# Turning softmax weights by VectorE and memory instead of by TensorE, in a two-layer decoder trunk

## The chip, the cores and the metric

The kernel runs on one NeuronCore of a Trainium2 chip. The metric is the device time of one execution in microseconds (us), the lower the better. Engines are named as in the profile: PE (TensorE, matrix products; PEld its weight loads), DVE (VectorE), ACT (ScalarE), POOL (GpSimd, which here only issues transfers), SP (which issues the transfers of the model's weights).

## The reference

Two layers over 256 tokens of width 2048, in fp32. The first layer has stick-breaking attention, the second, to which the change belongs, has dilated window attention in three groups of four heads over keys and values that are shared:

```
scores = einsum('brnqhd,brnkhd->brnhqk', qb, kb) * (dh ** -0.5)
scores = where(valid[:, None], scores, -inf)
m = max(scores, axis=-1);  e = exp(scores - m);  den = sum(e, axis=-1)
o = einsum('brnhqk,brnkhd->brnqhd', e / den, vb)
lse = m + log(den)
...
alpha = softmax(stack(lses, axis=2), axis=2)
o = stack(outs, axis=2) * alpha[..., None]
return o.reshape(b, s, B_WIDTH) @ w_o
```

So each head's output is its unscaled weights `e` times the values, times one factor per token, head and group (alpha over the denominator), and the 12 heads (1536 columns) go through `w_o`. After each attention follow a gated feed-forward block with a short convolution (5632 wide) and a gated addition of a per-layer embedding.

## The kernel before, in words

**Strips.** Every large product is made in strips of 512 output columns. `strip_v` keeps a strip in two PSUM banks, one for each half of the tokens (t = 0, 1), and for every block of 128 inputs and each half makes three products of 128x512: fp32 is rebuilt from a high and a low part of both sides (L346, L347, L348). A strip over 16 blocks is 96 such products. The model's weights come 1 MB at a time (`raw`, four buffers), and for every pair of blocks ScalarE writes the high part (`whi`, L303) and VectorE the low part (`wlo`, L304), with four buffers of each and priority over other work; a new pair can be written when TensorE is through with the pair four before.

**What sets the order.** The program is written without waits; a scheduler decides the order on each engine from the dependences, from the priorities and from `tc.issue_after`, which puts an instruction behind a given other one. Engines execute in that order.

**Turning.** A strip `u` with tokens on the partitions is turned (`turn_out`, `turn_in`) by VectorE in squares of 32x32 (L241), written to memory by POOL (`there<-y`, L244: two transfers of 256 KB) and read back with the squares rearranged (`turned<-there`, L252: four of 128 KB). The kernel does this for queries, keys and activations.

**The attention of the second layer** (`mixer_b`). Queries of groups 0 and 1, keys of groups 0 and 1, then `weights_of(0)`, queries of group 2, `weights_of(1)`, keys of group 2, values of group 0, `weights_of(2)`. `weights_of(g)` copies the turned queries into one run each on ScalarE (`in_one_run`, L487), makes the scores on TensorE into a double bank `two` (one buffer, queries of the second half) and a bank `keys` (first half), and for each head VectorE takes the maximum (L612, L613) and ScalarE the exponential (L614) into `e`, queries on the partitions, 384 columns: 256 for the second half of the queries, 128 for the first. Then a few small operations give the factors `co` (L637 to L649).

`weights_turned(g)` scales the four heads' `e` by `co` (L656), turns them on TensorE by 12 products with the identity `idf` (called through `one_run`, which is L406 in the profile), and copies the three banks out (L665, `aT`). `pv` multiplies: values are stationary, turned weights move; the result has the head's columns on the partitions, and is split into high and low parts as blocks `o` for the next product (L151, L152). This goes group by group between the strips of the values, and the strips of `wo_b` (12 blocks, 72 products each) follow in `add_strips`.

`products` makes a list of strips. With `late`, the first two strips are begun with the blocks that exist, `late()` is issued within the second of them to make the last four blocks, and then both are completed; in the kernel before, `wo_b` has no `late`.

Of the kernel before, what the change touches and what calls it, by code (L numbers as in the profile page):

```python
# [72 lines left out]
def tile_trunk(ctx, tc, head_d, xT_d, x_d, pT_d, pos_d, vec_d, cst_d, csb_d, wqkv, wo_a, wkv, wq_b, wo_b, wup, wdn, wpg, wpp, gfin_d, out_d):  # L73
# [277 lines left out]
    def products(jobs, xs, late=None, at=0, then={}):  # L351
# [6 lines left out]
        if late is not None:  # L358
            n = len(xs)

            def before(k0):
# [7 lines left out]
                strip_v(W, s, xs[:n], base, ends=False, before=(lambda k0: None, before)[i])  # L369
                for i, (W, s, base) in enumerate(jobs[:2])  # L370
# [3 lines left out]
            jobs = jobs[2:]  # L374
# [199 lines left out]
    def mixer_b(xs, late, hkv_of, rc):  # L574
# [15 lines left out]
        def weights_of(g):  # L590
            q, k = in_one_run(qs[g]), ks[g]
            gm = cbf[:, B_GM + g * S : B_GM + (g + 1) * S]
            two, one = two_banks(), bank("keys0")
            with one_run() as product:
# [10 lines left out]
                product(one.rearrange("p (h c) -> p h c", h=HG), IDB, mask, start=False, stop=True)  # L605
            for h in range(HG):
# [8 lines left out]
                es.append(e)  # L615
# [36 lines left out]
        def weights_turned(g):  # L652
            two, one = two_banks(), bank("keys1")
            for h, e in enumerate(es[g * HG : (g + 1) * HG]):
                for b, sl in ((1, slice(0, S)), (0, slice(S, S + P))):
                    nc.vector.tensor_scalar(e[:, sl], e[:, sl], co[:, b, g, h : h + 1], None, op0=OP.mult)  # L656
            with one_run() as product:
                for h in (3, 2, 1, 0):
                    e = es[g * HG + h]
                    keys0 = two[:, h // 2, (h % 2) * S : (h % 2 + 1) * S]  # L660
                    for out, c in ((keys0[:, :P], S), (keys0[:, P:], 0), (one[:, h * P : (h + 1) * P], P)):
                        product(out, e[:, c : c + P], idf, is_transpose=True, start=True, stop=True)
            ts = [rt("aT") for _ in range(3)]
            for t, d in zip(ts, (two[:, 0], two[:, 1], one)):
                nc.vector.tensor_copy(t, d)  # L665
            return [(ts[h // 2][:, (h % 2) * S : (h % 2 + 1) * S], ts[2][:, h * P : (h + 1) * P]) for h in range(HG)]

        heads = weights_turned(0)
        for g in range(NG):
            os += pv(heads, vs[g])  # L670
            if g + 1 < NG:
                heads = weights_turned(g + 1)
# [296 lines left out]
```

## Time and profile before

| | us |
|---|---|
| median of three runs | 2319.91 (2319.89 to 2320.4) |
| the profiled execution's own time | 2320.16 |
| its span, first to last instruction | 2318.4 |
| PE busy | 2303.9 |
| DVE, ACT, POOL busy | 1485.6, 1258.2, 267.6 |

Busy time counts an instruction from its start to its end; on TensorE successive products overlap, so the time that one takes from the next is read from the distance of their starts. A row of a timeline is: start, duration, engine, line, operation, output and inputs with buffer numbers left out, how many were merged, and in brackets the idle time before it and what ended it. The scores of the second layer's attention lie at 1297, 1322 and 1369 us of the span, the groups of products that the change removes at 1389, 1401 and 1414.

### The profile page before, as it was taken

Reading aid. Unit: us, or ns where it says so; the run is one execution under the profiler, and the core shown is the slowest. Engines: PE = TensorE matmul, PEld = TensorE weight load, DVE = VectorE, ACT = ScalarE, POOL = GpSimd, SP = SyncE. Lnnn points to the kernel's source line nnn. Section 1 sums busy time; section 2 is a strip of 40 time slices with the busy share of each in tenths; the row PEclk is TensorE's granted clock in tenths of the full one; section 3 lists DMA queues with packets and bytes.
Section 4 is the critical chain, followed back from the end, with each engine's and each line's share of the span. In section 5 each row is a group of like instructions: output and inputs, shape, how many; then the busy total and the mean of one; then the engine's idle time right before and its main releaser. Section 6 shows DMA issues by size and latency. Waiting matters only on the chain.

```text
span 2318.4 us, 27676 instructions
## 1 busy us (share of the span) xinstructions
PE 2303.9 (99%) x10268; PEld 1904.5 (82%) x10268; DVE 1485.6 (64%) x2110; ACT 1258.2 (54%) x1679; POOL 267.6 (12%) x466
## 2 busy tenths in 40 slices
PE   9999999999999999999999999999999999999998
PEld 7888888888888888888888888888888888888886
DVE  7555556677754767765677666667775476776565
ACT  6555545555544555545566544555553455654554
POOL 0100001111100111101011100211110011110100
PEclk9999999999999999999999999999999999999999
DMA  8656557677756777767677654867775677776763
GB/s 292 223 206 222 198 192 247 237 244 246 237 188 209 241 237 247 240 206 246 218 247 244 220 198 164 262 240 245 241 232 198 204 242 242 240 244 206 241 225 118
DMA packets 92168, 523.34 MB, mean 226 GB/s; under 512 B 14848, under 2 KB 15232, under 8 KB 40064
## 3 DMA queue, kind: packets, MB, share of 16 engines
q1 hardware_dynamic: 62352, 434.93, 53.3%
q0 software_dynamic: 27104, 80.77, 12.3%
q10 hardware_dynamic: 2576, 5.87, 0.7%
q8 instruction: 80, 1.31, 0.2%
q14 instruction: 56, 0.46, 0.1%
HBM read 479.04 MB, written 42.47 MB: 225 GB/s over the span
## 4 chain that ended last, share of the span: by engine, by line
PE 99%; DVE 0%; DMA 0%; ACT 0%; issue 0%; SPq 0%; DVEq 0%
PE accv L348 32%; PE accv L347 32%; PE accv L346 32%; PE two L406 2%; PE acc L330 1%; PE acc L333 0%; PE two L347 0%; PE two L346 0%; PE two L348 0%; DMA raw<-in_wqkv 0%; PE keys L406 0%; ACT whi L303 0%; DVE e L656 0%; DVE wlo L304 0%; ACT sq L215 0%
## 5 line engine op out<-in xcount | busy, mean ns | idle before, releaser
L304 DVE TENSOR_TENSOR wlo<-raw,whi 128x1024 fp32r<-128x1024 f32 (+1 forms) x821 | 1001.8, 1221 | 750.2 <-ACT whi L303 749.5
L303 ACT ACTIVATE whi<-raw 128x1024 fp32r<-128x1024 f32 (+1 forms) x821 | 867.4, 1058 | 908.8 <-PE accv L348 881.3
L348 PE MATMUL accv<-whi,h 128*128 128x512 f32 x2288 | 891.7, 390 | 0.0
L347 PE MATMUL accv<-wlo,h 128*128 128x512 f32 x2288 | 891.1, 389 | 0.0
L346 PE MATMUL accv<-whi,h 128*128 128x512 f32 x2288 | 890.5, 389 | 0.0
L348 PEld LDWEIGHTS accv<-whi,h 128*128 128x128 f32 x2288 | 429.5, 188 | 89.2
L347 PEld LDWEIGHTS accv<-wlo,h 128*128 128x128 f32 x2288 | 429.5, 188 | 88.9
L346 PEld LDWEIGHTS accv<-whi,h 128*128 128x128 f32 x2288 | 429.5, 188 | 88.8
L346 PE MATMUL accv<-whi,g 128*128 128x512 f32 x704 | 273.9, 389 | 0.0
L347 PE MATMUL accv<-wlo,g 128*128 128x512 f32 x704 | 273.9, 389 | 0.0
L348 PE MATMUL accv<-whi,g 128*128 128x512 f32 x704 | 273.9, 389 | 0.0
L244 POOL DMA_DIRECT2D there<-y x154 | 87.1, 566 | 1541.4 <-DVE y L241 1530.4
L252 POOL DMA_DIRECT2D turned<-there x308 | 180.3, 592 | 413.9 <-DMA there<-y 256.7
L347 PEld LDWEIGHTS accv<-wlo,g 128*128 128x128 f32 x704 | 132.1, 188 | 27.5
L346 PEld LDWEIGHTS accv<-whi,g 128*128 128x128 f32 x704 | 132.1, 188 | 27.5
L348 PEld LDWEIGHTS accv<-whi,g 128*128 128x128 f32 x704 | 132.1, 188 | 27.3
L346 PE MATMUL accv<-whi,o 128*128 128x512 f32 x224 | 87.4, 390 | 0.0
L348 PE MATMUL accv<-whi,o 128*128 128x512 f32 x224 | 87.3, 390 | 0.0
L347 PE MATMUL accv<-wlo,o 128*128 128x512 f32 x224 | 87.2, 389 | 0.0
L241 DVE STREAM_TRANSPOSE y<-u 128x512 f32<-128x512 f32 x114 | 80.3, 705 | 5.1 <-ACT u L383 2.6
L710 DVE SCALAR_TENSOR_TENSOR val<-turned,vec,val 128x248 f32<-128x248 f32 (+1 forms) x176 | 72.3, 462 | 0.0
L710 DVE SCALAR_TENSOR_TENSOR gate<-turned,vec,gate 128x240 f32<-128x240 f32 (+1 forms) x176 | 72.2, 461 | 0.0
(181 smaller groups left out, 1157.1 us busy)
## 6 DMA issues: line engine op xcount, KB each, us to landing
raw<-in_wup SPq DMA_DIRECT2D x176, 1024.0 KB, 5.2
raw<-in_wdn SPq DMA_DIRECT2D x88, 1024.0 KB, 4.9
raw<-in_wqkv SPq DMA_DIRECT2D x44, 1024.0 KB, 5.2
there<-y POOLq DMA_DIRECT2D x154, 256.0 KB, 3.9
turned<-there POOLq DMA_DIRECT2D x308, 128.0 KB, 4.9
raw<-in_wpg SPq DMA_DIRECT2D x32, 1024.0 KB, 4.9
raw<-in_wkv SPq DMA_DIRECT2D x24, 1024.0 KB, 5.1
raw<-in_wo_a SPq DMA_DIRECT2D x16, 1024.0 KB, 4.9
```

The lines of the kernel that those rows point to most:

```text
L241: last["turned"] = nc.vector.transpose(y.rearrange("p (b o r) -> p o b r", b=4, o=4), strip.rearrange("p (o b c) -> p o b c", o=4, b=4)).ins
L244: nc.gpsimd.dma_start(there[t * P : (t + 1) * P], y)
L252: nc.gpsimd.dma_start(z[32 * b : 32 * b + 32].rearrange("p a o r -> p a (o r)"), back[b])
L303: last["high"] = nc.scalar.activation(hi[:, c], r, AF.Copy).ins
L304: last["low weights"] = nc.vector.tensor_tensor(lo[:, c], r, f32(hi[:, c]), op=OP.subtract).ins
L330: nc.tensor.matmul(ps[o], hi[:, c], xs[k], start=k == 0, stop=False)
L346: nc.tensor.matmul(ps[t], xl, hi, start=k == 0 and not begun, stop=False)
L347: nc.tensor.matmul(ps[t], xh, lo, start=False, stop=False)
L348: nc.tensor.matmul(ps[t], xh, hi, start=False, stop=ends and k == n - 1)
L406: run.append(nc.tensor.matmul(*args, skip_group_check=True, **kw).ins)
L710: nc.vector.scalar_tensor_tensor(c, z[:, :, o, : 32 - d], taps(2 - d, j + o), c, op0=OP.mult, op1=OP.add)
```

## The change

The exponentials `e` are no longer scaled and no longer turned on TensorE. VectorE turns them in squares of 32x32 right after each head's exponentials (three operations a head, into three tiles `y`: the first and second half of the keys for the second half of the queries, and the keys of the first half), POOL writes each tile to memory (three transfers of 256 KB) and reads it back (twelve of 64 KB), and ScalarE copies each into one run per head (`weights_in_one_run`). For groups 0 and 1 these copies come at the head of the next `weights_of`, for group 2 behind the evacuation of the second strip of values.

In `values`, which replaces `pv`, the turned weights are stationary and the values move, 12 products of 128 columns a group, with queries on the partitions of the result. VectorE multiplies the result by `co` on its way out of PSUM, and the strip is turned through memory like the others; `split` then makes the `o` blocks from what came back. The last group's blocks are the `late` of `wo_b`, which begins three strips with the eight blocks of groups 0 and 1 before it completes them; the third lies in the double bank.

```diff
     def split(src, h):
-        nc.scalar.activation(h[:, :S], src, AF.Copy)
-        last["low"] = nc.vector.tensor_tensor(h[:, S:], src, f32(h[:, :S]), op=OP.subtract).ins
+        high, low = like(h[:, :S], src), like(h[:, S:], src)
+        nc.scalar.activation(high, src, AF.Copy)
+        last["low"] = nc.vector.tensor_tensor(low, src, f32(high), op=OP.subtract).ins
...
-    def products(jobs, xs, late=None, at=0, then={}):
+    def products(jobs, xs, late=None, at=0, then={}, side=2):
...
-                strip_v(W, s, xs[:n], base, ends=False, before=(lambda k0: None, before)[i])
-                for i, (W, s, base) in enumerate(jobs[:2])
+                strip_v(
+                    W,
+                    s,
+                    xs[:n],
+                    base,
+                    ends=False,
+                    before=before if i == side - 1 else lambda k0: None,
+                    room=two_banks() if i == 2 else None,
+                )
+                for i, (W, s, base) in enumerate(jobs[:side])
...
         def weights_of(g):
+            if g > 0:
+                weights_in_one_run(g - 1)
             q, k = in_one_run(qs[g]), ks[g]
...
+            ys = [rt("y") for _ in range(3)]
...
-                es.append(e)
+                squares = e[:, : 3 * P].rearrange("p (k b r) -> p k b r", k=3, b=4)
+                for k in range(3):
+                    y = ys[k].rearrange("p (b h r) -> p h b r", b=4, h=HG)
+                    nc.vector.transpose(y[:, h], squares[:, k])
+            zs = []
+            for y in ys:
+                there = dram.tile([P, 512], F32, tag="weights", bufs=3, name=nm("there"))
+                nc.gpsimd.dma_start(there, y)
+                zs.append((rt("turned"), there))
+            for z, there in zs:
+                back = there.rearrange("(a c) (b f) -> b c a f", c=32, b=4)
+                for b in range(4):
+                    nc.gpsimd.dma_start(z[32 * b : 32 * b + 32].rearrange("p (a f) -> p a f", a=4), back[b])
+            es.append([z for z, _ in zs])
+
+        def weights_in_one_run(g):
...
+            for z in es[g]:
+                r = rt("run")
+                with tc.issue_after(last["out"]), tc.issue_after(last["high"]):
+                    nc.scalar.activation(
+                        r.rearrange("p (h a r) -> p h a r", h=HG, r=32), z.rearrange("p (a h r) -> p h a r", h=HG, r=32), AF.Copy
+                    )
+                out.append(r)
+            es[g] = out
...
-        def weights_turned(g):
-            two, one = two_banks(), bank("keys1")
-            for h, e in enumerate(es[g * HG : (g + 1) * HG]):
-                for b, sl in ((1, slice(0, S)), (0, slice(S, S + P))):
-                    nc.vector.tensor_scalar(e[:, sl], e[:, sl], co[:, b, g, h : h + 1], None, op0=OP.mult)
...
-                    for out, c in ((keys0[:, :P], S), (keys0[:, P:], 0), (one[:, h * P : (h + 1) * P], P)):
-                        product(out, e[:, c : c + P], idf, is_transpose=True, start=True, stop=True)
...
-        heads = weights_turned(0)
-        for g in range(NG):
-            os += pv(heads, vs[g])
...
+        def values(g, v):
...
+                for t, parts in ((1, ((w[1], v[1]), (w[0], v[0]))), (0, ((w[2], v[0]),))):
+                    for i, (wt, vt) in enumerate(parts):
+                        for h in (3, 2, 1, 0):
...
+                            product(po[:, t, c], wt[:, c], vt[:, c], start=first, stop=final)
...
+                nc.vector.tensor_tensor(heads(u), heads(po[:, t]), c, op=OP.mult)
...
+            return turn_in(turn_out(us))
...
+        z = values(0, vs[0])
+        vs.append(scaled(strip_v(wkv, NG + 1, hkv), rc, lambda: rt("v")))
+        weights_in_one_run(2)
+        zs = [z, values(1, vs[1])]
+
+        def before(k0):
+            if k0 == len(hkv) - 2:
+                with tc.issue_after(last["high"]), tc.issue_after(last["low weights"]):
+                    use(zs[0])
+
+        vs.append(scaled(strip_v(wkv, NG + 2, hkv, before=before), rc, lambda: rt("v")))
+        with tc.issue_after(last["out"]), tc.issue_after(last["low weights"]):
+            use(zs[1])
+        z = values(2, vs[2])
+        return os, lambda: use(z)
...
-        h, late = add_strips(wo_a if i == 0 else wo_b, o, G_FFN + i * KB, norm)
+        h, late = add_strips(wo_a if i == 0 else wo_b, o, G_FFN + i * KB, norm, late=o_late, at=4, side=3)
```

How this moves instructions is read from the order on each engine. The first place is TensorE at group 0's weights (in these rows a name ends with its tile's number; L406 is the line of `one_run` before and L415 after, L346 to L348 become L347 to L349). Before, the end of a value strip, the turning products and, 14 products later, the value products:

```order
L348 MATMUL accv_10931<-whi_11024,h_9789 128x512
L406 MATMUL two_10841<-idf,e_10252 128x128 x2
L406 MATMUL keys_1982_10842<-idf,e_10252 128x128
L406 MATMUL two_10841<-idf,e_10245 128x128 x2
L406 MATMUL keys_1982_10842<-idf,e_10245 128x128
L406 MATMUL two_10841<-idf,e_10238 128x128 x2
L406 MATMUL keys_1982_10842<-idf,e_10238 128x128
L406 MATMUL two_10841<-idf,e_10231 128x128 x2
L406 MATMUL keys_1982_10842<-idf,e_10231 128x128
L346 MATMUL accv_10924<-whi_11040,h_9792 128x512
```

After, at the corresponding place:

```order
L347 MATMUL accv_11003<-whi_11078,h_9721 128x512
L348 MATMUL accv_11003<-wlo_11079,h_9721 128x512
L415 MATMUL two_10961<-v_10852,run_10461 128x128 x4
L415 MATMUL two_10961<-v_10850,run_10459 128x128 x4
L415 MATMUL two_10961<-v_10850,run_10463 128x128 x4
L349 MATMUL accv_11003<-whi_11078,h_9721 128x512
L347 MATMUL accv_11003<-whi_11078,h_9724 128x512
```

The turning products and their two PSUM tiles are gone, and the value products stand alone between strip products.

The second place is ScalarE ahead of the scores of group 1. Before, the strip of group 2's queries is evacuated (`u`, L383) and the queries of group 1 are copied into runs:

```order
L303 ACTIVATE whi_10508<-raw_10506 128x1024
L383 ACTIVATE u_10397<-accv_10265,rq_9478 128x512
L303 ACTIVATE whi_10524<-raw_10506 128x1024
L383 ACTIVATE u_10399<-accv_10272,rq_9478 128x512
L487 ACTIVATE run_10423<-turned_9879 128x256 x2
L487 ACTIVATE run_10426<-turned_9879 128x256 x2
L303 ACTIVATE whi_10542<-raw_10540 128x1024
```

After:

```order
L392 ACTIVATE u_10435<-accv_10308,rq_9478 128x512
L648 ACTIVATE run_10459<-turned_10276 128x512
L648 ACTIVATE run_10461<-turned_10279 128x512
L304 ACTIVATE whi_10620<-raw_10618 128x1024
L304 ACTIVATE whi_10636<-raw_10618 128x1024
L648 ACTIVATE run_10463<-turned_10282 128x512
L496 ACTIVATE run_10465<-turned_9879 128x256 x2
L496 ACTIVATE run_10468<-turned_9879 128x256 x2
L304 ACTIVATE whi_10654<-raw_10652 128x1024
```

Three copies of weights that came back from memory, and two more weight pairs, now stand ahead of the query copies (L487, now L496).

The third place is TensorE at the scores that wait for these copies. Before, they stand behind the second product of the strip's second weight pair (`whi_10490`; the strip's first is `whi_10472`):

```order
L348 MATMUL accv_10483<-whi_10472,h_9590 128x512
L346 MATMUL accv_10476<-whi_10490,h_9593 128x512
L347 MATMUL accv_10476<-wlo_10491,h_9593 128x512
L406 MATMUL two_10429<-turned_10207,run_10426 128x256
L406 MATMUL keys_1914_10430<-turned_10207,run_10426 128x128
```

After, they stand behind the first product of its fourth pair (`whi_10602`; the pairs are `whi_10550`, `whi_10568`, `whi_10586`, `whi_10602`):

```order
L349 MATMUL accv_10561<-whi_10586,h_9602 128x512
L347 MATMUL accv_10554<-whi_10602,h_9709 128x512
L415 MATMUL two_10471<-turned_10207,run_10468 128x256
L415 MATMUL keys_1926_10472<-turned_10207,run_10468 128x128
L415 MATMUL two_10471<-turned_10207,run_10468 128x256
```

A pair is 12 products, so the scores moved from behind 14 products of the strip to behind 37, 23 later. In the same way the scores of group 2 stand 11 strip products later than before. From the end of `wo_b`'s third strip on, TensorE's order is that of before.

More of the change, by code (lines that the diff above doesn't have):

```diff
@@ new lines, in use @@
+        def use(z):
+            for h in range(HG):
+                o = rt("o", dt=F32R)
+                split(z[:, :, h], o)
+                os.append(o)
+        z = values(0, vs[0])
[6 more added lines that the diff above has]
+                    use(zs[0])
```

32 lines of the change are left out of this document (16 added, 16 removed).

## The prediction

> **What bounds the kernel now.** I read the page's busy shares and its chain of work first, then TensorE's waits, then its timeline around the lines that the change touches.
>
> ```profile
> PE 2303.9 (99%) x10268; PEld 1904.5 (82%) x10268; DVE 1485.6 (64%) x2110; ACT 1258.2 (54%) x1679; POOL 267.6 (12%) x466
> ...
> PE 99%; DVE 0%; DMA 0%; ACT 0%; issue 0%; SPq 0%; DVEq 0%
> ```
>
> TensorE (PE) carries the end: the chain that ended last is TensorE for 99%. Its waits, in us in total, times, longest:
>
> ```profile
> PE acc L330 <- DVE h L146: 2.0, 3, 1.2
> PE warm L127 <- DVE zero L124: 1.2, 1, 1.2
> PE two L406 <- DVE e L656: 0.2, 1, 0.2
> ```
>
> Only the last lies in the changed part. So a microsecond is won only where TensorE gets less to do, and lost where it meets a wait it did not have; VectorE, ScalarE and GpSimd count only through such a wait. The windows say how much room they have (columns: TensorE, weight loads, VectorE, ScalarE, GpSimd, granted clock, DMA share, GB/s):
>
> ```profile
> 1310.00:1330.00 20.00, 20.00 (x95) 16.46 (x94) 12.94 (x27) 10.82 (x22) 2.46 (x5) 1.00 0.54 188
> ...
> 1390.00:1410.00 20.00, 20.00 (x106) 17.02 (x105) 15.12 (x32) 7.10 (x12) 0.00 (x0) 1.00 0.44 159
> ```
>
> **What the removed turning costs TensorE.** The timeline of TensorE (start, duration) around the three groups; durations overlap, so I use starts:
>
> ```profile
> 1388.39 0.39 PE L348 MATMUL accv<-whi,h 128*128 128x512 f32 x1
> 1388.99 0.41 PE L406 MATMUL two<-idf,e 128*128 128x128 f32 x2 [0.21 <-DVE e L656]
> ...
> 1390.56 0.39 PE L347 MATMUL accv<-wlo,h 128*128 128x512 f32 x1
> ...
> 1393.32 0.39 PE L347 MATMUL accv<-wlo,h 128*128 128x512 f32 x1
> 1393.55 2.78 PE L406 MATMUL two<-aT,v 128*128 128x128 f32 x16
> ...
> 1396.40 0.40 PE L346 MATMUL accv<-whi,h 128*128 128x512 f32 x1
> ...
> 1401.17 0.39 PE L346 MATMUL accv<-whi,h 128*128 128x512 f32 x1
> ...
> 1403.11 0.40 PE L348 MATMUL accv<-whi,h 128*128 128x512 f32 x1
> ...
> 1406.07 0.39 PE L346 MATMUL accv<-whi,h 128*128 128x512 f32 x1
> ...
> 1409.14 0.40 PE L348 MATMUL accv<-whi,h 128*128 128x512 f32 x1
> ...
> 1413.69 0.39 PE L347 MATMUL accv<-wlo,h 128*128 128x512 f32 x1
> ...
> 1415.51 0.40 PE L346 MATMUL accv<-whi,h 128*128 128x512 f32 x1
> ...
> 1424.59 0.39 PE L347 MATMUL accv<-wlo,o 128*128 128x512 f32 x1
> ...
> 1427.85 0.40 PE L346 MATMUL accv<-whi,o 128*128 128x512 f32 x1
> ```
>
> The pace of the strips comes from 1396.40 to 1401.17: 21 products, 0.227 us each. The first strip product behind an insertion starts before the pipeline has settled, so I go to the second one, two paces on. The 12 turning products of group 0 cost 1390.56 - 1388.39 - 2 x 0.227 = 1.72 us (with the 0.21 of waiting), of group 1 1403.11 - 1401.17 - 0.45 = 1.49, of group 2 1415.51 - 1413.69 - 0.45 = 1.37. All 36 go: **-4.57 us**. Their VectorE neighbours (L656, L665) go too, which frees no time of TensorE beyond that wait.
>
> The value products cost in the same way 2.63, 2.62 and 2.81 us. Before, 8 products of 128 or 256 columns, 1536 columns in all, each in two passes (the x16). After: 12 products of 128 columns, the same 1536, in 24 passes. Equal columns give +0. The turning products are passes of 128 columns too: (1390.56 - 0.23 - 1388.99)/12 = 0.112 each, and 24 of these are 2.69, 0.07 more. Could the weight loads hold short passes up? One lasts 0.188 (the last number but one in its group's row is the mean in ns):
>
> ```profile
> L348 PEld LDWEIGHTS accv<-whi,h 128*128 128x128 f32 x2288 | 429.5, 188 | 89.2
> ```
>
> Held up, the eight short passes of before would take 1.5 us, and with 0.22 for each long one the group 3.3; it took 2.62, and with 0.112 and 0.22 it is 2.69. So they don't. I take **+0.15** for three groups, between 0 and +0.21. The extra 0.19 of group 2 (its wait for values or weights) may go or stay: I let it stay.
>
> VectorE's turning against TensorE's is where a page of the Trainium skill speaks against the change: "VectorE: DVE Perf Modes", Rules for kernel authors, advises TensorE for a full 128x128 turn where PSUM will do as its goal, and The three transpose paths gives 390 ns for it there. By that price the 36 would be worth 14.0 us (an estimate), and the time 2306.9; the three stretches above contain all 36 and hold 4.57, and the measurement decides. That the other way costs more than it saves is rival C.
>
> **A new wait before the scores of group 1.** The weights of group 0 now go VectorE, memory, back, and three ScalarE copies. The new order puts these copies ahead of the copies of the queries that the scores of group 1 wait for, and these scores 23 strip products later. What stood there before, in TensorE's timeline (scores of group 0, scores of group 1, the second strip product behind them) and ScalarE's:
>
> ```profile
> 1297.43 0.64 PE L406 MATMUL two<-turned,run 128*128 128x256 f32 x2
> ...
> 1322.54 0.64 PE L406 MATMUL two<-turned,run 128*128 128x256 f32 x2
> ...
> 1326.09 0.40 PE L346 MATMUL accv<-whi,h 128*128 128x512 f32 x1
> ```
> ```profile
> 1309.03 0.19 ACT L614 ACTIVATION_READ_ACCUMULATOR e<-keys,nmx 128x1 f32 x1
> ...
> 1319.57 1.06 ACT L303 ACTIVATE whi<-raw 128x1024 fp32r<-128x1024 f32 x1 [0.67 <-PE accv L348]
> 1320.54 0.67 ACT L383 ACTIVATE u<-accv,rq 128x512 f32<-128x512 f32 x1
> 1321.10 1.33 ACT L487 ACTIVATE run<-turned 128x256 f32<-128x256 f32 x4
> 1322.33 1.05 ACT L303 ACTIVATE whi<-raw 128x1024 fp32r<-128x1024 f32 x1
> ```
>
> TensorE reaches the scores at 1322.54 + 23 x 0.227 = 1327.76. ScalarE, from 1321.10: two copies of 128x512 from SBUF (0.62 each by the row below), a weight pair that TensorE frees at 1322.33, the next one at 1322.33 + 12 x 0.227 = 1325.05, done at 1326.1, the third copy to 1326.7, and the four query copies to 1328.0; before, TensorE started 0.11 behind them (1321.10 + 1.33 to 1322.54). So 1328.1, a wait of **0.35** even if memory is never late.
>
> ```profile
> L215 ACT ACTIVATE sq<-x 128x512 f32<-128x512 f32 x48 | 29.9, 623 | 1.1 <-DVE x L821 0.4
> ```
>
> Is it late? The rows for the way through memory, before, in GpSimd's timeline, VectorE's group of such turns, and the landing of transfers into the turned tiles between 1300 and 1360:
>
> ```profile
> 1298.79 0.56 POOL L244 DMA_DIRECT2D there<-y  x1 [2.19 <-DVE y L241]
> 1303.25 2.34 POOL L252 DMA_DIRECT2D turned<-there  x4 [3.90 <-DMA there<-y]
> ...
> 1451.57 2.35 POOL L252 DMA_DIRECT2D turned<-there  x4 [5.16 <-DMA there<-y]
> ```
> ```profile
> L241 DVE STREAM_TRANSPOSE y<-u 128x512 f32<-128x512 f32 x114 | 80.3, 705 | 5.1 <-ACT u L383 2.6 <-DMA there<-y 2.2
> ```
> ```profile
> DMA to landing us min/median/max: 2.7/3.2/5.4
> ```
>
> The last exponentials ended at 1309.2. VectorE now turns three 128x128 squares for each of four heads: a quarter of the row's 0.705 is 0.18, and a fixed part makes it more; I take 0.27, so 0.8 a head and at most 3.2 in all, part of it in VectorE's idle time: ready at 1311 to 1312.4, taken 1311.6. The first copy out to the first copy back is 4.46 us (1298.79 to 1303.25), and up to 0.56 + 5.16 = 5.7 in the busier row: 1316.1. Twelve issues back at 2.34/4 = 0.585: the last begins at 1322.5 and lands 2.7 to 5.4 later (the pieces are half the bytes), 3.2 in the middle: 1325.7 against the 1326.1 at which ScalarE gets there. Hidden, then, by a margin of 0.4 only; with the long values 1316.1 + 1.3 + 6.4 + 5.4 = 1329.2, 3.1 over. The earlier two tiles, waited for too, can push the two weight pairs by up to 1 us. I take **0.7** for the whole wait, with ends 0 and 3.4. What queues behind the waiting copies on ScalarE are weight pairs; TensorE needs the next one only after the scores and 11 strip products (1326.09 - 0.23 - 1322.54 + 11 x 0.227 = 5.8 us), so they starve nothing below some 5 us.
>
> **Scores of group 2.** They stand 11 strip products later, and three copies and one weight pair go ahead of the query copies:
>
> ```profile
> 1367.98 1.32 ACT L487 ACTIVATE run<-turned 128x256 f32<-128x256 f32 x4
> ```
> ```profile
> 1369.42 0.64 PE L406 MATMUL two<-turned,run 128*128 128x256 f32 x2
> ```
>
> TensorE: 1369.42 + 11 x 0.227 = 1371.92. ScalarE: 1367.98 + 3 x 0.57 + 1.0 + 1.32 + 0.11 = 1372.1. **+0.2**, between 0 and 0.5. Memory is no part of it: from scores to return the way of group 0 takes 1325.7 - 1297.4 = 28 us, and the scores of groups 1 and 2 lie 44 apart. Those of group 2 have 175 strip products, 40 us, before their weights are used.
>
> **What I cost at nothing.** (1) The outputs' way (scaling by VectorE out of PSUM, turn, memory, splits): those of groups 0 and 1 have a whole strip of 96 products (21.8 us) and more; those of group 2 have three strips of 8 blocks, 144 products, 32.7 us, against about 1.4 + 1.4 + 4.5 + 2.3 + 5.4 + 2 = 17. Without that cover each us over is a us of TensorE. (2) The third strip takes the double bank, free once group 2's products are scaled, 16 us before. (3) Strips 0 to 2 of wo end 5.4 us apart instead of 16.3, so VectorE's additions and turns bunch; weight pairs go ahead of them in both queues, and the fourth strip (72 products, 16.3 us) takes the rest. (4) The extra traffic, 9 x 0.5 + 3 x 1 MB over 130 us, is 58 GB/s on DMA engines busy for 0.44 to 0.54.
>
> **Sum:** -4.57 + 0.15 + 0.7 + 0.2 = -3.5 us. The profiled execution took 2320.16, so 2316.6; it lies 0.25 above the median 2319.91, so a median of **2316.4**. A measurement tells about 0.2% (4.6 us) from no change: faster begins at 2315.3, slower at 2324.6.
>
> **Rivals.** *A, memory is late* (13%): the scores of group 1 wait 2 to 4 us, as with the long values above; for it speaks that twelve small pieces follow each other on one queue where the row has four; against it the median. 2317.7 to 2319.7. One sentence on its cause: "SBUF — State Buffer", SBUF: two separate sides, says that some VectorE operations lock GpSimd out from writing descriptors; GpSimd's issues above, 0.56 to 0.59 each beside a VectorE busy for 64%, show none of it. *B, nothing is late* (9%): no new wait, equal products, and group 2's 0.19 gone: -4.57 - 0.19 = -4.8, 2315.2. Against it speaks the copy chain, which is longer by more than the 23 products without memory. *C, slower* (4%): the same copies on ScalarE as in A, but the return so late that weight pairs starve behind it. Every us beyond 1326.1 costs one: the gain is eaten by a return at 1330.0 (-4.57 + 0.15 + 0.35 + 0.2 = -3.9), and a loss of over 4.6 needs 1334.6, a landing of 12 us where the longest seen took 5.4. There TensorE also runs out of weight pairs. 2324.6 and more. That the turning is still on TensorE can't be: the order of after has none of its rows.
>
> **Chances.** Forecast (2315.3 to 2317.7) 74%, A 13%, B 9%, C 4%. Range: from B's 2315.1 to A's 2318.8, leaving out the end of A and C. Faster by over 0.2%: B and the forecast's lowest end, 0.11. Slower: 0.04. Same: 0.85.
>
> **What would show it.** No products with idf on TensorE; each group of value products at 2.6 to 2.9 us; a gap of 0.3 to 1.5 us before the scores of group 1, released by a ScalarE run copy, and one under 0.5 before group 2's; none at the o blocks of wo. It is wrong if TensorE waits anywhere else, above all for weight pairs behind a late copy, or if the scores of group 1 wait over 2 us.

## The result and the profile after

| | us |
|---|---|
| before, median of 4 runs | 2320.15 (2319.89 to 2320.96) |
| after, median of 4 runs | 2334.16 (2332.43 to 2336.05) |
| after over before | 1.0061, 95% interval 1.0049 to 1.0073 |
| the profiled execution of after | 2336.05, span 2333.9 |
| predicted | 2316.4 |

The change made the kernel slower by 14 us. The busy shares and the chain of work in the page of after:

```profile
PE 2306.9 (99%) x10256; PEld 1906.7 (82%) x10256; DVE 1488.5 (64%) x2125; ACT 1262.6 (54%) x1688; POOL 302.8 (13%) x529
...
PE 96%; DMA 2%; DVE 1%; issue 0%; ACT 0%; POOL 0%; SPq 0%; DVEq 0%; ACTq 0%; POOLq 0%
```

TensorE is still the bound, but DMA now has 2% of the chain, so something in memory sets the end for a while. What TensorE waited for in after (total, times, longest, in us):

```profile
PE two L415 <- ACT run L496: 6.7, 1, 6.7
PE two L415 <- DMA turned<-there: 5.2, 1, 5.2
```

L415 is what L406 was. These two single waits stand before the scores of group 1 and of group 2. TensorE's timeline of after at both places:

```profile
1329.56 0.39 PE L347 MATMUL accv<-whi,h 128*128 128x512 f32 x1
1336.63 1.22 PE L415 MATMUL two<-turned,run 128*128 128x256 f32 x2 [6.69 <-ACT run L496]
...
1338.08 1.06 PE L415 MATMUL two<-turned,run 128*128 128x256 f32 x2
...
1343.11 0.39 PE L349 MATMUL accv<-whi,h 128*128 128x512 f32 x1
...
1383.50 0.39 PE L347 MATMUL accv<-whi,h 128*128 128x512 f32 x1
1389.10 1.19 PE L415 MATMUL two<-turned,run 128*128 128x256 f32 x2 [5.21 <-DMA turned<-there]
...
1394.94 0.39 PE L349 MATMUL accv<-whi,h 128*128 128x512 f32 x1
```

Two losses at each place. The pause: 1336.63 - 1329.56 - 0.23 = 6.8 us and 1389.10 - 1383.50 - 0.23 = 5.4. And the pace behind it: from the scores' start to the second strip product behind them 6.48 us in group 1 and 5.84 in group 2, where the kernel before needed 1326.09 - 1322.54 = 3.55; that is 2.9 and 2.3 more. The windows of after show why (columns as before):

```profile
1330.00:1336.00 6.00, 0.00 (x0) 0.00 (x0) 2.08 (x2) 3.88 (x8) 1.42 (x3) 0.69 0.44 145
1336.00:1344.00 8.00, 7.37 (x24) 5.94 (x25) 2.32 (x6) 1.89 (x4) 2.34 (x4) 0.59 0.74 197
1344.00:1354.00 10.00, 10.00 (x45) 8.26 (x44) 8.24 (x27) 6.32 (x20) 0.05 (x1) 1.00 0.28 107
...
1389.00:1395.00 6.00, 5.91 (x21) 4.96 (x22) 0.31 (x1) 0.00 (x0) 0.00 (x0) 0.60 0.25 105
```

The granted clock falls while TensorE stands still (0.69 over the first pause), averages 0.59 and 0.60 of full speed over the scores that follow, and is 1.00 again behind them. It is at half from 1332.31 to 1342.55 and from 1386.92 to 1393.75; the rows are in the last section.

The sum: 6.8 + 2.9 + 5.4 + 2.3 = 17.4 us lost at the scores. Behind the scores of group 2 the kernel is 3.8 us shorter than before: its last product comes 928.07 us after the last product of those scores, 934.39 in before, and 11 strip products (2.5 us) have moved ahead of them. The scores of group 0 begin 2.0 us later (1299.46 against 1297.43), from waits at the start of the kernel that the change doesn't touch. 17.4 - 3.8 + 2.0 = 15.6, and the profiled executions differ by 15.9.

What the first pause waited for, in ScalarE's timeline of after:

```profile
1329.56 0.63 ACT L648 ACTIVATE run<-turned 128x512 f32<-128x512 f32 x1 [6.33 <-DMA turned<-there]
1332.32 0.63 ACT L648 ACTIVATE run<-turned 128x512 f32<-128x512 f32 x1 [2.12 <-DMA turned<-there]
1332.85 1.99 ACT L304 ACTIVATE whi<-raw 128x1024 fp32r<-128x1024 f32 x2
1334.74 0.61 ACT L648 ACTIVATE run<-turned 128x512 f32<-128x512 f32 x1
1335.26 1.32 ACT L496 ACTIVATE run<-turned 128x256 f32<-128x256 f32 x4
```

ScalarE stands at the copies of group 0's weights (L648), and the query copies (L496) that the scores need stand behind them; the releaser is a transfer into `turned`. GpSimd's timeline of after shows the way through memory, and for group 1 what came behind it:

```profile
1313.61 1.65 POOL L634 DMA_DIRECT2D there<-y  x3 [6.08 <-DVE y L630]
1320.52 4.36 POOL L639 DMA_DIRECT2D turned<-there  x8 [5.26 <-PE accv L349]
1328.14 2.17 POOL L639 DMA_DIRECT2D turned<-there  x4 [3.25 <-DMA turned<-there]
...
1361.26 4.36 POOL L639 DMA_DIRECT2D turned<-there  x8 [5.64 <-DMA there<-y]
1367.82 2.17 POOL L639 DMA_DIRECT2D turned<-there  x4 [2.20 <-PE accv L349]
1369.98 1.11 POOL L245 DMA_DIRECT2D there<-y  x2
1378.33 2.34 POOL L253 DMA_DIRECT2D turned<-there  x4 [7.24 <-DMA there<-y]
```

Out to back took 6.9 us: the first transfer out landed 6.3 us after its issue, and the return was issued 0.6 later. (The return's row names TensorE, which ended a product just then; with the same three tiles in the kernel before, below, the row names the transfer.) Then eight of the twelve pieces were issued, GpSimd waited 3.3 us until an earlier one had landed, and the last four followed. The keys of group 2 (L245, L253) are issued without idle time behind the weights of group 1. They had been standing behind them, for VectorE had turned their second half by 1360.6, 9.4 us before the first of these issues:

```profile
1359.88 0.71 DVE L242 STREAM_TRANSPOSE y<-u 128x512 f32<-128x512 f32 x1
```

They were back at 1389.

### The profile page after: what moved, and what is told of

It reads as the page before. It is cut to its first block, busy times and chain, and to the rows that moved or that the text cites. A ratio compares the mean times of both kernels' runs of the same rounds, so it can differ in the third digit from the quotient of the medians.

```text
span 2333.9 us, 27792 instructions
## 1 busy us (share of the span) xinstructions
PE 2306.9 (99%) x10256; PEld 1906.7 (82%) x10256; DVE 1488.5 (64%) x2125; ACT 1262.6 (54%) x1688; POOL 302.8 (13%) x529
## 4 chain that ended last, share of the span: by engine, by line
PE 96%; DMA 2%; DVE 1%; issue 0%; ACT 0%; POOL 0%; SPq 0%; DVEq 0%; ACTq 0%; POOLq 0%
PE accv L347 30%; PE accv L348 30%; PE accv L349 30%; PE two L415 2%; DMA turned<-there 1%; DMA there<-y 1%; PE acc L331 1%; PE two L347 0%; PE two L348 0%; PE two L349 0%; PE acc L334 0%; DMA raw<-in_wqkv 0%; PE keys L415 0%; POOL turned L253 0%; ACT whi L304 0%
## 5 line engine op out<-in xcount | busy, mean ns | idle before, releaser
L348 PE MATMUL accv<-wlo,h 128*128 128x512 f32 x2288 | 891.3, 390 | 0.0
L349 PE MATMUL accv<-whi,h 128*128 128x512 f32 x2288 | 891.2, 390 | 0.0
L347 PE MATMUL accv<-whi,h 128*128 128x512 f32 x2288 | 890.5, 389 | 0.1
L347 PEld LDWEIGHTS accv<-whi,h 128*128 128x128 f32 x2288 | 429.5, 188 | 89.3 <-DVE h L146 0.5
L349 PEld LDWEIGHTS accv<-whi,h 128*128 128x128 f32 x2288 | 429.5, 188 | 89.1
L348 PEld LDWEIGHTS accv<-wlo,h 128*128 128x128 f32 x2288 | 429.4, 188 | 89.1 <-issue 0.2
L245 POOL DMA_DIRECT2D there<-y x160 | 90.6, 567 | 1430.4 <-DVE y L242 1408.4
L347 PE MATMUL accv<-whi,g 128*128 128x512 f32 x704 | 273.9, 389 | 0.0
L348 PE MATMUL accv<-wlo,g 128*128 128x512 f32 x704 | 273.9, 389 | 0.0
L349 PE MATMUL accv<-whi,g 128*128 128x512 f32 x704 | 273.9, 389 | 0.0
L253 POOL DMA_DIRECT2D turned<-there x320 | 187.6, 593 | 439.2 <-DMA there<-y 222.1
L349 PEld LDWEIGHTS accv<-whi,g 128*128 128x128 f32 x704 | 132.1, 188 | 27.6
L347 PEld LDWEIGHTS accv<-whi,g 128*128 128x128 f32 x704 | 132.1, 188 | 27.4
L348 PEld LDWEIGHTS accv<-wlo,g 128*128 128x128 f32 x704 | 132.1, 188 | 27.3
L347 PE MATMUL accv<-whi,o 128*128 128x512 f32 x200 | 78.0, 390 | 0.0
L349 PE MATMUL accv<-whi,o 128*128 128x512 f32 x200 | 77.9, 389 | 0.0
L348 PE MATMUL accv<-wlo,o 128*128 128x512 f32 x200 | 77.8, 389 | 0.0
```

Of the source, the lines that this page charges most:

```text
L245: nc.gpsimd.dma_start(there[t * P : (t + 1) * P], y)
L253: nc.gpsimd.dma_start(z[32 * b : 32 * b + 32].rearrange("p a o r -> p a (o r)"), back[b])
L347: nc.tensor.matmul(ps[t], xl, hi, start=k == 0 and not begun, stop=False)
L348: nc.tensor.matmul(ps[t], xh, lo, start=False, stop=False)
L349: nc.tensor.matmul(ps[t], xh, hi, start=False, stop=ends and k == n - 1)
```

## The experiments

Theory Q: the whole loss is two queues, ScalarE's (query copies behind copies whose weights are late) and GpSimd's (keys behind weights). Rival D: the DMA engines are full, so whatever the order, something is late. Rival S: the scores are slow of themselves. "Before" beside each is from runs on the same chip.

**The copies later, the keys first, both.**

```diff
         def weights_of(g):
-            if g > 0:
-                weights_in_one_run(g - 1)
             q, k = in_one_run(qs[g]), ks[g]
...
             es.append([z for z, _ in zs])
+            if g > 0:
+                weights_in_one_run(g - 1)
```

> One edit to the kernel after: the copies of group g-1's weights into runs stand behind the exponentials of group g instead of ahead of its query copies; the scores of groups 1 and 2 move back to the places they had before. Theory Q (two queues, two waits): the wait before the scores of group 1 is ScalarE standing in its queue at a copy whose weights are not yet back, and the scores run at half pace because TensorE was idle ahead of them. So the wait of 6.7 us goes, those scores take about 3.55 us again instead of 6.5, and the time falls by 9 to 10 us to about 2324.5; the scores of group 2 still wait 5 us for their keys. Rival D (the DMA engines are full): the transfers are late because the engines are, and the 7 us for which TensorE stood gave the loads time to catch up; without them the keys of group 2 come later against TensorE, their wait grows to 8 us or more, and the time falls by under 6 us, to 2328 or more. Rival S (the scores are slow of themselves in the new order, from where their operands lie): they stay at 6 us or more without a wait ahead of them.

In the second, the lines with the fifteen transfers (L632 to L640 of after) become a function `send`, which `weights_of` calls for groups 0 and 2 alone and which puts each transfer out behind the last return of a strip issued so far:

```diff
-        weights_of(1)
+        ys1 = weights_of(1)
         ks.append(turned(strip_v(wkv, 2, hkv), rc))
+        send(ys1)
```

> One edit to the kernel after: on GpSimd's queue the fifteen transfers of group 1's weights are issued behind the way of the keys of group 2 instead of ahead of it. Theory Q: the keys are back before TensorE asks for them, the wait of 5.2 us before the scores of group 2 goes, these take about 3.55 us instead of 5.8, and the time falls by 7 to 8 us to about 2326.5; the scores of group 1 keep their 6.7 us. Rival D: the bytes are the same and the engines busy for over 0.9 of this stretch, so the keys' transfers still land in 6 us or more each, and 2 us or more of the wait stay; 2329 or more. A third outcome: the weights of group 1, now later, make ScalarE wait at their copies ahead of the scores of group 2, so that the wait only changes its name; 2334 then.

> Both edits at once. Theory Q: no wait at any scores, all three groups of scores at 3.5 us, and the gain of 4.6 us that the removed turning is worth comes out: about 2316, 4 us under the kernel before. Rival D: with neither pause the loads and the turns need more than the engines give, a wait of 2 us or more stays somewhere in the stage; 2319 to 2326.

Measured: copies later 2319.64 (2316.71 to 2324.73, ten runs; ratio to before 1.0, 0.9991 to 1.0009). Keys first 2334.83 (1.0064, 1.005 to 1.0078). Both 2317.82 (0.9993, 0.9984 to 1.0002), which is the time of the kernel before and no clear gain over it. With the copies later no scores wait, and all three groups take 3.09 us from their first to their last product, as in before (group 1 took 6.03 in after): S falls, for the same scores on the same operands are quick once no pause stands ahead of them. The time falls further than Q said, because the second pause went as well. With the keys alone first, TensorE waits for the copies of both groups instead:

```profile
PE two L415 <- ACT run L496: 9.7, 2, 6.8
PE accv L347 <- DVE o L153: 2.2, 1, 2.2
PE acc L331 <- DVE h L146: 2.2, 3, 0.9
PE accv L347 <- DVE h L146: 1.8, 1, 1.8
```

That is the third outcome of its expectation: the second pause changed its name, from the keys to the weights of group 1, and was 2.9 us long. So as long as copies stand ahead of query copies, the queue's order can't win.

**The traffic alone, and the traffic with the copies.** Into the kernel before:

```diff
                 es.append(e)
+                squares = e[:, : 3 * P].rearrange("p (k b r) -> p k b r", k=3, b=4)
+                for k3 in range(3):
+                    y = ys[k3].rearrange("p (b h r) -> p h b r", b=4, h=HG)
+                    nc.vector.transpose(y[:, h], squares[:, k3])
+            for y in ys:
...
+                nc.gpsimd.dma_start(there, y)
...
+                    nc.gpsimd.dma_start(z[32 * b : 32 * b + 32].rearrange("p (a f) -> p a f", a=4), back[b])
```

> The kernel before, with only the new traffic put in: for each group VectorE turns the unscaled exponentials in squares and GpSimd writes the three tiles and reads them back, in the place that they have in the kernel after, and nothing uses what comes back; the turning on TensorE and all else stay. Theory Q: the scores of group 1 meet no wait, since no copy on ScalarE waits for the tiles; the keys of group 2 still stand behind the fifteen transfers in GpSimd's queue, so the scores of group 2 wait about 5 us and then run slowly for 5.8 us: 2320.2 + 7.7 = about 2328. Rival D: the traffic hurts weight loads too, there are waits for weight pairs, and it is 2328 or more with waits at the strips. If the first pause of the kernel after was what made the keys late, there is no wait here: 2320.

```diff
         def weights_of(g):
+            for z in held.pop(g - 1, []):
+                r = rt("run")
+                with tc.issue_after(last["out"]), tc.issue_after(last["high"]):
+                    nc.scalar.activation(
...
             q, k = in_one_run(qs[g]), ks[g]
```

> The kernel before with the full ballast and one thing more: ScalarE copies the tiles that came back into runs ahead of the query copies of the next group, as in the kernel after; the scores of group 1 and 2 move to the later places of after; nothing uses the copies, and the turning on TensorE, pv and wo are those of before. Theory Q says that these six copies at this place are the whole loss: scores of group 1 wait 6 to 7 us and then take 6.5, those of group 2 wait about 5 and take 5.8, so 2320.2 + 17.4 = about 2337. If the loss needs another part of the change (the value products, the three strips of wo, the turned outputs), it is 2320 to 2326.

Traffic alone: 2320.72 (2319.75 to 2326.56, ten runs; 1.0002, 0.9993 to 1.0011), no wait for memory on TensorE; its DMA engines are busy for 0.91 to 0.97 of 1330 to 1370, more than before's 0.54 to 0.83, and nobody feels it. Rival D falls as a cause by itself. Q's 2328 falls too: the keys stand behind the weights here as in after, and are in time by some 1 us (back by 1368.1, asked for at 1369.2). Its expectation's last sentence held here: without the first pause the second is gone. With so thin a margin that isn't always so; copies later with two strips, below, has 1.2 us of it without a first pause. Traffic with the copies: 2331.74 (1.0054, 1.0037 to 1.0071), 11.6 us over before, with TensorE's waits

```profile
PE two L406 <- ACT run L487: 6.4, 1, 6.4
...
PE two L406 <- DMA turned<-there: 1.2, 1, 1.2
```

and scores of group 1 that take 4.81 us instead of 3.09. Six copies at that place, in a kernel that has nothing else of the change but its traffic, bring the first pause nearly in full. The second is 1.2 here and 5.2 in after, and the scores of group 2 aren't slow behind it (3.12 us). So the loss lies between the two outcomes of its expectation: 11.6 of the 17.4 us. It needs no other part of the change, but what it lacks is the second pause.

**Why the weights are late.** The traffic-alone kernel with one tile instead of three (`for y in ys[:1]`), and with whole tiles back:

> The kernel before with a third of the new traffic: of the three tiles only the first is written and read back (1 + 4 transfers a group instead of 3 + 12), unused. It tells what makes the way out slow: with all three tiles 7.2 us from the first issue out to the first issue back, where the two outs of the queries' way took 4.5. If it is the kernel's own bytes in the queue, 4.5 us or less with one tile. If it is the loads of weights that run at the same time, 6 us or more again. Time as before, 2320.

```diff
-                for b in range(4):
-                    nc.gpsimd.dma_start(z[32 * b : 32 * b + 32].rearrange("p (a f) -> p a f", a=4), back[b])
+                nc.gpsimd.dma_start(z, there)
```

> The kernel before with the same bytes as the full ballast, but each tile comes back in one transfer of 256 KB with rows of 2 KB instead of four of 64 KB with runs of 512 bytes (so nothing is rearranged; nobody uses it). With the small pieces group 0's first issue back was at 1318.5, the last issue ended at 1327.2, and it landed some 5 us later. If the many small pieces are what is slow (twelve issues, the wait for a free place in the queue, short runs), the last tile is back by 1326. If the engines are simply full of bytes, the three tiles land in 8 us or more and the last is back at 1329 or later. Time as before, 2320.

2320.26 and 2319.28, one run each, so the parts below are read from one trace each. GpSimd's timeline with all three tiles in small pieces:

```profile
1311.35 1.65 POOL L624 DMA_DIRECT2D there<-y  x3 [6.12 <-DVE y L620]
1318.54 4.35 POOL L629 DMA_DIRECT2D turned<-there  x8 [5.54 <-DMA there<-y]
1325.00 2.17 POOL L629 DMA_DIRECT2D turned<-there  x4 [2.11 <-DMA turned<-there]
```

with one tile, and with three whole tiles, whose landing stands below it:

```profile
1311.77 0.57 POOL L624 DMA_DIRECT2D there<-y  x1 [5.98 <-DVE y L620]
1317.81 2.17 POOL L629 DMA_DIRECT2D turned<-there  x4 [5.46 <-PE accv L348]
```
```profile
1318.31 1.71 POOL L627 DMA_DIRECT2D turned<-there  x3 [5.86 <-DMA there<-y]
...
DMA to landing us min/median/max: 5.0/5.2/6.0
```

The way out takes 7.2 us with three tiles and still 6.0 with one: of the 2.7 us above the 4.5 that I had taken, 1.5 are there with a third of the bytes, beside the loads of that stretch, and 1.2 are the kernel's own bytes. Of the way back the small pieces are the greater part: whole tiles are all issued by 1320.0 and back by 1319.5 + 6.0 = 1325.5; in small pieces the last one is only issued at 1326.6 and lands no sooner than 1330.9 (4.3 was the shortest landing there). Fewer and larger pieces that do rearrange the squares would need a larger tile, for which SBUF had no room; they weren't tried.

The same edit in the kernel after:

> The kernel after, with each tile of weights read back in one transfer of 256 KB with rows of 2 KB instead of four of 64 KB; so the return doesn't rearrange the squares, and the attention's weights are in the wrong places. The order on TensorE then has the scores of group 1 twelve strip products earlier than after has them. If the many small pieces make the return late, as the ballast says (last tile back 5.5 us sooner), ScalarE's third copy ends at about 1328 and the scores, asked for at 1327, wait 1 to 2 us instead of 6.7, run at 3.6 us, and those of group 2 wait little or not at all: 2316 to 2319. If it is only the bytes and the loads beside them, the wait is 5 us or more and the time 2330 or more.

2327.37 in one run. The wait is 3.3 us, between the two expectations; the weights were back by 1325, as Q said, but with the scores twelve products earlier TensorE asked at 1324.5, and a weight pair and the query copies came behind the last weights' copy. The scores ran slowly even behind 3.3 us (6.02 us), and those of group 2 didn't wait. The time lies between the expectations too; waits of 1.2, 0.9 and 0.8 us at the start of the feed-forward block are part of it. So small pieces made the weights late, but with the copies where they are even an early return leaves a pause.

**Two strips of wo instead of three.** Both edits left one new wait, for blocks h at the start of the feed-forward block: 1.0 us, and 2.4 with the copies alone moved.

```diff
-        h, late = add_strips(wo_a if i == 0 else wo_b, o, G_FFN + i * KB, norm, late=o_late, at=4, side=3)
+        h, late = add_strips(wo_a if i == 0 else wo_b, o, G_FFN + i * KB, norm, late=o_late, at=4, side=2)
```

> Both edits as before, and wo begins with two strips instead of three, as every other product with late blocks does. The kernel with both edits still waits 1.0 us once at the first strip of the feed-forward block, for blocks h, and with the copies alone moved 2.4 us there: the strips of wo end bunched, their turns queue behind each other on GpSimd, and the third strip's blocks come late. If that is the third strip's doing, the strips end apart again, this wait is gone, and the time is 1 to 2 us under that of both edits: about 2316. Rival: with 96 products of cover instead of 144 the blocks of group 2 are late for wo; from the trace of both edits they are there at about 1440 and TensorE asks at 1443, so a wait of 0 to 3 us there, 2318 to 2320.

> The copies moved behind the exponentials, and wo begun with two strips; the weights' transfers of group 1 stay ahead of the keys' way on GpSimd's queue. It tells whether the reordering of that queue is worth anything once the copies are out of the way. In the trace with the copies alone moved, the keys of group 2 were issued back at 1361 to 1363.4 and TensorE asked at some 1370, so no wait if they land within 6 us: then 2316, like both edits with two strips. If the margin is too small, some executions wait there for 1 to 3 us, and the median is 2317 to 2319 with a wide spread.

Both edits with two strips: 2315.86 (2315.35 to 2317.06, eleven runs), ratio 0.9983, 0.9974 to 0.9992, 3.9 us under the kernel before and under both kernels of this study. Its longest wait is the one at the start of the kernel:

```profile
PE acc L331 <- DVE h L146: 1.4, 2, 0.8
```

The three strips did cost that wait. Without the reordered queue (copies later, two strips) it is 2319.56 (2316.49 to 2325.62; 1.0002, 0.9993 to 1.0011), with 1.2 us for the keys and 0.8 for o blocks in the profile: once the copies are gone from ScalarE's queue, the order on GpSimd's is worth 3.7 us in the median and most of the spread.

**The strips alone in the kernel after**, and after itself once more on one chip:

> The kernel after with only the last part undone: wo begins with two strips instead of three. If the two pauses at the scores are the whole loss, as the sum of the trace says (17.4 us of pauses and slow scores against 4.6 saved), it stays at 2334, within 1.5. If the three strips of wo and the bunched turns behind them take part in the loss of this kernel, it falls by 2 us or more.

> The kernel after, unchanged, beside the next one on the same chip. Up to wo both have the same order of instructions on every engine, yet the kernel with two strips took 2327.6 (2324.9 to 2331.7) where after took 2334.2 (2332.4 to 2336.1), and its trace has the gain ahead of wo: 1.6 us in the first pause with its slow scores, 5.3 in the second. If that is chance from execution to execution (the moment at which transfers meet the loads of weights), this kernel spreads over 2325 to 2336 too and the medians of the two lie within 3 us. If the programs differ in earnest, it stays at 2332 to 2336.

> The kernel after with two strips at the head of wo, once more beside after on the same chip. By chance: within 3 us of it. In earnest: 2325 to 2331 again, some 6 us under it.

Two strips alone: 2327.57 (2324.87 to 2331.68), again 2329.71 (2324.61 to 2331.26); after again 2334.19 (2325.83 to 2337.99, six runs; 1.0056 of before, 1.0042 to 1.007). After spreads by 12 us where before spreads by one. Its profile here is of the fastest execution, 2325.83:

```profile
PE two L415 <- ACT run L496: 6.9, 1, 6.9
...
PE two L415 <- ACT v L392: 0.3, 1, 0.3
```

The first pause is as long as ever, the second is missing, in the same program. So the second is a near miss that comes and goes between executions of one program. The medians of two and three strips still lie 4.5 us apart, more than the 3 that I had set for chance, and this is **open**: behind the scores of group 2 the profiles of both end within 1.2 us of each other (927.65 and 928.82 against 928.07), and ahead of wo both have one order of instructions.

## Why the prediction was wrong

**The turning.** -4.57 was right as far as it can be seen. (The 2.69 given for the mixed passes of before is 2.66 by its own figures, which changes nothing.) The value products cost more than +0.15. In after's timeline (strip product, group 0, two strip products):

```profile
1404.25 0.39 PE L348 MATMUL accv<-wlo,h 128*128 128x512 f32 x1
1404.48 2.94 PE L415 MATMUL two<-v,run 128*128 128x128 f32 x24
...
1407.50 0.39 PE L347 MATMUL accv<-whi,h 128*128 128x512 f32 x1
```

1407.50 - 1404.25 - 0.45 = 2.80, and 2.77 and 2.87 in groups 1 and 2, against 2.63, 2.62 and 2.81: +0.38. With some 0.3 at a late block of the feed-forward block at 1517 that gives about the 3.8 us saved. In the best version above the whole way from the scores of group 0 to the last product is 1005.47 us, in before 1009.47.

**The wait before the scores of group 1** is the term that failed: 0.7, with ends 0 and 3.4, against 6.8 + 2.9. The step "the last begins at 1322.5 and lands 2.7 to 5.4 later" put the third tile back at 1325.7. After is 2.0 later there from its start, so 1327.7; it was back by 1334.74. The 7.0 us are three parts: out to back 6.9 instead of 4.46 (+2.4); the twelve issues, whose last began 9.2 us behind the first instead of 6.4, since after eight of them GpSimd waited 3.25 for a landing (+2.8); and up to 5.0 from that issue to the copy instead of 3.2 (+1.8). All three durations I took from turns that are four pieces alone on their queue, in a stretch whose DMA engines were busy for 0.54; a median of there was used for a stage that the change itself fills (0.83 there in after):

```profile
DMA to landing us min/median/max: 4.6/6.9/8.0
```

is the landing of the twelve pieces in after. "By a margin of 0.4 only" was in the text; what it missed is that the margin's own terms grow together. Point (4), that the traffic costs nothing, was right as the traffic-alone kernel has it, and was then wrongly taken to hold for a wait behind that traffic. Point (3), that the bunched strips cost nothing, failed by 1 to 2.4 us, which showed only once the pauses were gone.

**A pause costs more than its length.** Every rival counted a microsecond of waiting as one microsecond. The half clock behind the pauses adds some 40% here (5.2 to 12.2 us). "TensorE: Matmul & The Clock Gate" of the Trainium skill, Part 1 (What's actually happening), has a free-running window of some 3.4 us and half the clock after an idle one; here the stretches at half pace fit it (below), but pauses shorter than the window have set one off, so as a bound on harmless pauses the measurement decides against it.

**The scores of group 2.** "Memory is no part of it" failed. I compared the way of the weights with the 44 us between two scores, and not the way of the keys, which these scores need and which now stands behind fifteen issues on GpSimd's queue. What is queued behind the added instructions was asked on ScalarE alone, not on GpSimd. The wait was 0 to 5.2 us, and most of it grows out of the first: the scores of group 1 come later, so the weights of group 1 are sent later (1353.95 in after, 1337.20 with the copies later), while the keys are asked for only 13.8 us later (1383.7 against 1369.9). The rest is how long the transfers take: the four pieces of keys landed 7.8 to 8.9 us after their issue in after, where 2.9 to 7.3 in after again left no wait for them, and 7.7 to 8.3 in copies later with two strips brought 1.2 us without any first pause.

**The rivals.** A named the right mechanism, small pieces one after another on one queue, and priced it at 4 us at most. C ended on the right side by another way: no weight pairs were missed, and a landing of 12 us wasn't needed, as 7 us came from three terms together. **Nothing at the o blocks** and **no idf products** held.

## What to carry to other kernels

When work is sent through memory, ask not only when it is back but what stands behind it: on the queue that issues the transfers, and on the engine that takes the result, ahead of work that others wait for. Put such a consumer behind the urgent work, not ahead of it with a thin margin; here that place was worth 14 us. Take a transfer's landing from a stage as busy as the one that the change makes, count small pieces by number and not only by bytes, and price a pause of TensorE at more than its length: those of 2.9 us and more cost 1.7 to 2.9 us on top here, and of those between 1.77 and 2.4 us some cost 1.6 or so and some nothing.

## What the hardware showed that I had not expected

A pause far shorter than those at the scores can cost half the clock too. With the keys first, at the start of the feed-forward block:

```profile
1516.06 0.50 PE L347 MATMUL accv<-whi,h 128*128 128x512 f32 x1 [1.84 <-DVE h L146]
1516.40 0.58 PE L348 MATMUL accv<-wlo,h 128*128 128x512 f32 x1
...
1519.33 0.63 PE L349 MATMUL accv<-whi,h 128*128 128x512 f32 x1
1519.75 0.45 PE L347 MATMUL accv<-whi,h 128*128 128x512 f32 x1
```

From 1516.40 to 1519.75, 3.4 us, products come every 0.43 us instead of 0.23: 1.84 us of pause cost 1.6 more. The window over them has a granted clock of 0.52:

```profile
1516.30:1519.70 3.40, 3.40 (x9) 2.67 (x9) 2.98 (x8) 2.28 (x3) 2.34 (x4) 0.52 0.92 281
```

With the copies later a pause of 2.40 brought the same 3.4 us (1503.38 to 1506.78), beginning 1.06 us after TensorE had started again. Pauses of 1.04, 1.15, 1.18, 2.20 and 2.21 us brought none. So not the length alone decides, but also where the pause falls, and the granted clock of after shows how. Between its start-up and its last product it is at half in three stretches, and each of them comes with a pause. The first pause stands ahead of the whole attention, at the start of the kernel:

```profile
11.09 1.45 PE L331 MATMUL acc<-h,whi 128*128 128x512 f32 x3 [1.77 <-DVE h L146]
```
```profile
11.35:14.76 3.41, 3.41 (x12) 2.83 (x12) 3.24 (x7) 3.41 (x7) 0.00 (x0) 0.50 1.04 414
...
1332.31:1342.55 10.24, 5.92 (x18) 4.81 (x19) 3.58 (x3) 5.21 (x9) 2.34 (x4) 0.50 0.61 177
...
1386.92:1393.75 6.83, 4.66 (x14) 4.06 (x15) 0.00 (x0) 0.00 (x0) 0.00 (x0) 0.50 0.52 187
```

The stretches last one, three and two times 3.413 us, and between them lie 1317.55 and 44.37 us, which is 386 and 13 times 3.413. With the keys first, 47.79 and 126.30 us lie between the stretches at half clock, 14 and 37 times. So in these traces the clock changes only at fixed steps of 3.413 us. The pauses of 1.77, 1.84 and 2.40 us each lay within one step (the first from 9.33 to 11.09, in the step from 7.93 to 11.35) and brought half the clock from the next step on; hence the 1.06 us of full speed behind the 2.40. Those of 2.20 and 2.21 us were cut by a step's end, at 1441.36 and 1381.42, with 1.84 and 1.73 us in the larger part. What seems to count is how much of one step TensorE stands idle, with a bound at about half of it. That is read from traces and wasn't tried by itself, and where exactly the bound lies stays open, as 1.84 us stands on both sides.
